# Earlier features for the next head pair, and another spacing of the background products, in a one-core diffusion layer

## The chip, the cores and the metric

One core of a Trainium2 chip. The metric is the device time of one execution in microseconds (us); less is better. TensorE does the matrix products (its clock is granted at one of two levels, 1.2 and 2.4 GHz), VectorE (DVE) and ScalarE (ACT) the elementwise work, GpSimd (POOL) some of it, and SyncE (SP) issues the transfers.

## The reference, cut to what matters

One layer for 256 latent tokens and 256 context tokens of width 2048. A wide input projection feeds two token mixers, RWKV-7 in both directions (16 heads of 64) and differential attention (8 heads); two sigmoid gates of width 2048 merge them, and a mixture of 32 experts follows.

```
px = hx @ w_in[l]                      # 3712 RWKV columns, 3072 attention columns, 4096 gate columns
S  = S * w_t - (S @ kk_t) (kk_t * a_t) + v_t k_t        # per head, forward and backward; y_t = S @ r_t
a  = softmax(q0 k0) - lam * softmax(q1 k1);  o = a @ v  # per attention head
gates = sigmoid(p_gate)
mixed = gates[0] * (y_rwkv @ w_pa) + gates[1] * (y_diff @ w_pb)
out = (silu(xb @ w1[e]) * (xb @ w3[e])) @ w2[e]         # experts, last
```

## The kernel before

The recurrence is done in chunks of 64 tokens. The 16 heads go as four pairs of pairs, q = 0 to 3; a q holds an even and an odd pair of heads (o = 0 and 1). For each q there are four stages:

- `feats`, that is `feat` for the even and then for the odd pair: loads, three small products (`pk`, `pw`, `pa`), sigmoids on ScalarE, a scan and products on VectorE and GpSimd. They give the tiles `P0`, `P1`, `R` and `kq` of the pair.
- `within`: products inside the chunks (`pc`, `px`), masked into `A` and `M`, and transposes (`pq`).
- `deltas`: first `inverse`, a substitution of 31 steps on VectorE (`prod`, then a sum into `z`), two transposes by VectorE (`ZT`, `Z`), then products of 32x32 blocks (`ph`, `pz`); beside it the side generator (transposes `pp`, `pv`, products `pb`). Then the products `pW`, `pu`, `pG`, and the chain of seven states (`pS`, then `state` on VectorE).
- `tail`: normalisation and the store of the result.

In `deltas`, `ahead(n)` emits n pieces of `feats(q + 1)`. Before, all of the next features stand behind the inverse.

All of this is the foreground. The background is one long list of weight products (L486 and L517): the attention's inputs, the keys, values and receptances (`kvr`), and at the end the gates (128 parts of 12 matmuls each, 128x128 by 128x256), then the merge with the attention's result. A weight part is loaded in 256 KB, split into `whi` (ScalarE) and `wlo` (VectorE, or GpSimd where `self.low` says so, which is during the inverse), and multiplied in 12 or 24 matmuls. Each piece of the foreground yields a weight; `interleave` multiplies it with a scale and `fill` emits background steps until their own weights (0.65 for 6 matmuls) have used it up:

```
def fill(self, us):
    self.credit += us
    while self.credit > 0 and self.at is None:
        w = self.step()
        if not isinstance(w, str):
            self.credit -= w
```

The scales are 0.936 for `diff` (the attention), 1.234 for the first `feats` and 0.444 for the four q. So a larger weight puts more background ahead of the foreground's next piece. What is emitted earlier has priority, but the framework that builds the kernel places an instruction on its engine when it takes it to be ready; the order on each engine is then fixed. Tiles with the same tag share a buffer: `b0` to `b3` hold `kq` of the even (0, 1) and of the odd pair (2, 3) and are reused in the inverse.

Of the kernel before, what the change touches and what calls it, by code (L numbers as in the profile page):

```python
# [9 lines left out]
F32 = mybir.dt.float32  # L10
# [8 lines left out]
P = 128  # L19
# [181 lines left out]
class Body:  # L201
# [793 lines left out]
    def feats(self, q):  # L995
        self.ce = self.rwt("ce", [P, 2, 2, NC], 2)

        self.vv = self.rwt("vv", [P, NC, 2, C])
        self.pts = [self.rwt(f"P{d}", [P, NC, 2, C]) for d in range(2)]
        a = yield from self.feat(2 * q)  # L1000
        b = yield from self.feat(2 * q + 1)
        return a, b
# [190 lines left out]
    def deltas(self, st, q):  # L1193

        nc, K, pt = self.nc, self.K, self.pts
        pst, tl, ident = self.pst, self.rwt, self.ident
        FW, FG, FC, FO = (0.1, 0.1, 0.1, 0.1) if q < 3 else (0.7, 0.7, 0.7, 0.7)
        W = self.rb.tile([P, 2 * NC, P], F32, tag="W", name="W")
# [9 lines left out]

        side = side()
        self.low = nc.gpsimd  # L1210
        for n, w in enumerate(self.inverse([s["A"] for s in st])):
            if n % 2:
                next(side, None)
            yield w * (1.0 if q < 3 else 0.731)
        for _ in side:
            pass
        self.low = None

        fe, nxt = (self.feats(q + 1) if q < 3 else iter(())), [None]

        def ahead(n):
            for _ in range(n):
                try:
                    w = next(fe)
                except StopIteration as e:
                    if e.value is not None:
                        nxt[0] = e.value
                    return
                if isinstance(w, str):
                    yield w  # L1230

        for dc in range(0, 2 * NC, 4):
# [23 lines left out]
        for i0, ni in ((0, 4), (4, 2)):  # L1256
            pg = [pst("pG") for _ in range(2)]
            for i in range(ni):
                for d, c in enumerate(order[i0 + i + 1]):
                    for h in range(2):  # L1260
                        for s in st:
                            o, us = s["o"], H2[1 - s["o"]]
                            n = (2 * i + d) * C
# [53 lines left out]
        for i in range(NC - 1):  # L1317
            pn = added(i + 1) if i < NC - 2 else None
            sn = state[:, (i + 1) % 4]
            if i:  # L1320
                so = state[:, i % 4]
                for h in range(2):
                    prev = None
                    for s in st:
                        o = s["o"]
                        for d in range(2):
                            n = (2 * o + d) * C
# [78 lines left out]
    def inverse(self, As):  # L1406

        nc, tl, pst = self.nc, self.rwt, self.pst
        NB = 2 * NC * 2
        Av = [A.rearrange("p d c h t -> p (d c h) t") for A in As]  # L1410

        na = tl("na", [P, 32, 32], tag="b0")
        z = tl("z", [P, 32, 32], tag="b1")
        prod = tl("prod", [P, 32, 32], tag="b2")
        rows = self.rows
        nc.vector.transpose(na.rearrange("b s t -> b t s"), self.dg16.rearrange("p d n t -> p t (d n)"))
        yield 1.5
        nc.gpsimd.memset(z, 0.0)
# [8 lines left out]
        nc.vector.transpose(ZT.rearrange("p n s -> p s n"), z.rearrange("b t s -> b s t"))  # L1427
        Z = self.rb.tile([P, NB, 32], F32, tag="s", name="Z")
        nc.vector.transpose(Z.rearrange("p n t -> p t n"), z)
        yield 3.077  # L1430

        for g in range(2):
            ph = [pst("ph") for _ in range(2)]
            for o in range(2):
                r0, r1 = rows(o, 0), rows(o, 1)
                for n in range(16):
                    m = g * 16 + n
                    nc.tensor.matmul(ph[o][r1, n * 32:n * 32 + 32], Av[o][r0, m, 32:64], ZT[r0, m, :],
                                     start=True, stop=True, tile_position=(r0.start, r1.start))
                nc.scalar.copy(H[r1, g * 16:g * 16 + 16], ph[o][r1, :].rearrange("p (n t) -> p n t", n=16))  # L1440
            yield 0.7
            pz = [pst("pz") for _ in range(2)]
            for o in range(2):
                r0, r1 = rows(o, 0), rows(o, 1)
                for n in range(16):
                    m = g * 16 + n
                    nc.tensor.matmul(pz[o][r0, n * 32:n * 32 + 32], H[r1, m, :], Z[r1, m, :],  # L1447
                                     start=True, stop=True, tile_position=(r1.start, r0.start))
                nc.scalar.copy(Av[o][r0, g * 16:g * 16 + 16, 32:64], pz[o][r0, :].rearrange("p (n t) -> p n t", n=16))
                nc.scalar.copy(Av[o][rows(o, g), :, 32 * g:32 * g + 32], Z[rows(o, g)])  # L1450
            yield 0.7

# [7 lines left out]
    def diff(self):  # L1460
# [5 lines left out]
        def tl(name, shape, bufs=1, tag=None):  # L1466
            return df.tile(shape, F32, tag=tag or name, name=name, bufs=bufs)
# [33 lines left out]
        def prepare(h):  # L1501
# [26 lines left out]
            nc.vector.tensor_tensor(flat(ro[:, 0:4, :]), flat(qk[:, 0:4, :]), ct.rearrange("p a m d -> p (a m d)"), ALU.mult)  # L1528
            yield 0.7
            nc.gpsimd.tensor_tensor(ro[:, 4:6, :].rearrange("p a (m d) -> p (a m) d", m=2),  # L1530
# [18 lines left out]
        def attend(h, qT, kT, vt):  # L1549
            oT = tl("o", [P, T])  # L1550
            for t in range(2):
                ts = slice(t * P, t * P + P)
                pm, r = [], []
                for m in range(2):
                    sc = pst("sc")
                    nc.tensor.matmul(sc, qT[:, m, ts], kT, start=True, stop=True)
                    yield 0.7
                    mx = tl("mx", [P, 1], 4)
# [4 lines left out]
                    nc.scalar.activation(p, sc, AF.Exp, scale=0.125, bias=mx, accum_out=sm)  # L1563
                    yield 0.7
                    nc.vector.reciprocal(sm, sm)
# [10 lines left out]
                nc.scalar.copy(aT, pa.rearrange("p (k q) -> p k q", k=4))  # L1576
                yield 0.7
                po = pst("po")
# [391 lines left out]
```

## Time and profile before

| | |
|---|---|
| median of 3 runs | 2506.11 us (2496.79 to 2522.02) |
| profiled execution | 2509.57 us, its span 2507.6 us, mean granted clock 0.973 |
| TensorE busy | 2346.5 us, 94% of the span |
| VectorE, ScalarE, GpSimd busy | 48%, 32%, 9% |
| attention (`diff`) | about 310 to 500 us |
| first features, then keys and values alone | about 500 to 720 us |
| q = 0, 1, 2, 3 | about 720 to 880, 880 to 1040, 1040 to 1190, 1190 to 1330 us |
| merge, output projection, router | 1330 to 1550 us |
| experts | from 1550 us on |

Busy is the share of time in which an engine has an instruction under way. The granted clock is 1 at 2.4 GHz and 0.5 at 1.2 GHz; a value between is a mean over a stretch that holds both.

### The profile page before, as it was taken

The page shows a single profiled execution, that of the slowest core. Times are in us where ns is not written, and L with a number is a line of the kernel's source. Part 1 is how long each engine was busy: PE and PEld are TensorE (multiplying, and loading weights), DVE is VectorE, ACT ScalarE, POOL GpSimd, SP SyncE. Part 2 cuts the span into 40 slices and gives each one's busy share as a digit, 9 for nine tenths or more (in the row PEclk, how much of TensorE's full clock was granted, in tenths as well). Part 3 has the DMA queues.
Part 4 walks back from the last instruction along what each step waited for, and adds up shares of the span by engine and source line. Part 5 has one row for each costly group of instructions (what it writes and reads, how often), then busy time and mean ns, then how long its engine had stood idle before and what let it go on. Part 6 is the DMA issues. An engine that isn't in the chain of part 4 may idle for free.

```text
span 2507.6 us, 45450 instructions
## 1 busy us (share of the span) xinstructions
PE 2346.5 (94%) x18419; PEld 1654.6 (66%) x18419; DVE 1204.9 (48%) x2239; ACT 796.6 (32%) x1479; POOL 219.7 (9%) x279
## 2 busy tenths in 40 slices
PE   6999989899999899999999898999999999999997
PEld 3799977788998687787899876444444434443442
DVE  3355677778655674766745654222222222222223
ACT  3332345455354655656534442000000000000000
POOL 0110012113113332102000000000000000000000
PEclk9999999999998998989889999999999999999999
DMA  9977764567754332353438897799999999999997
GB/s 348 340 243 242 238 204 138 168 206 242 231 156 124 106 115 77 122 163 100 132 116 253 257 322 273 319 421 421 420 421 421 420 421 421 421 421 421 421 421 323
DMA packets 233127, 691.50 MB, mean 276 GB/s; under 512 B 34840, under 2 KB 72400, under 8 KB 182864
## 3 DMA queue, kind: packets, MB, share of 16 engines
q1 hardware_dynamic: 232912, 688.54, 74.3%
q8 instruction: 146, 2.39, 0.4%
q14 instruction: 69, 0.57, 0.1%
HBM read 666.66 MB, written 21.78 MB: 275 GB/s over the span
## 4 chain that ended last, share of the span: by engine, by line
PE 50%; DMA 31%; DVE 8%; issue 5%; ACT 3%; POOL 2%; SPq 1%; DVEq 0%; ACTq 0%; POOLq 0%
DMA w<-in_exp_w_dram 17%; PE acc L486 12%; PE acc L517 6%; DMA r<-in_exp_w_dram 5%; PE pa L1821 5%; PE po L1856 4%; PE pt L1753 3%; PE acc L811 3%; DMA raw<-in_ws_dram 3%; DMA d<-in_exp_w_dram 2%; DVE wlo L965 1%; PE pc L1128 1%; PE ada L647 1%; PE pu L1247 1%; PE pz L1447 1%
## 5 line engine op out<-in xcount | busy, mean ns | idle before, releaser
L1821 PE MATMUL pa<-w,hg 128*64 128x512 f32 x1408 | 390.2, 596 | 35.0 <-DMA w<-in_exp_w_dram 31.8
L964 ACT CAST whi<-raw 128x512 fp32r<-128x512 f32 (+1 forms) x463 | 280.1, 614 | 310.7 <-PE acc L486 148.4
L965 DVE TENSOR_TENSOR wlo<-raw,whi 128x512 fp32r<-128x512 f32 (+1 forms) x420 | 289.4, 704 | 85.2 <-ACT whi L964 79.9
L1821 PEld LDWEIGHTS pa<-w,hg 128*64 128x64 f32 x1408 | 119.8, 137 | 245.5 <-issue 178.0
L486 PE MATMUL acc<-xr,whi 128*128 128x256 f32 (+1 forms) x1248 | 269.7, 294 | 0.7 <-ACT whi L964 0.7
L486 PE MATMUL acc<-xd,whi 128*128 128x256 f32 (+1 forms) x1248 | 267.2, 291 | 0.3 <-DVE g L750 0.2
L486 PEld LDWEIGHTS acc<-xr,whi 128*128 128x128 f32 (+1 forms) x1248 | 209.0, 195 | 20.0 <-issue 17.6
L486 PEld LDWEIGHTS acc<-xd,whi 128*128 128x128 f32 (+1 forms) x1248 | 206.3, 192 | 18.3 <-issue 14.1
L1768 DVE TENSOR_TENSOR hm<-hm,pa 128x512 f32<-128x512 f32 x16 | 11.0, 688 | 417.9 <-PE pa L1821 417.9
L1856 PE MATMUL po<-w,hT 128*64 128x512 f32 (+1 forms) x712 | 191.9, 587 | 1.6 <-DMA w<-in_exp_w_dram 0.9
L486 PE MATMUL acc<-xr,wlo 128*128 128x256 f32 (+1 forms) x624 | 182.7, 293 | 4.4 <-DVE wlo L965 3.9
L486 PE MATMUL acc<-xd,wlo 128*128 128x256 f32 (+1 forms) x624 | 181.5, 291 | 1.6 <-DVE wlo L965 1.6
L603 DVE SCALAR_TENSOR_TENSOR ada<-raw,cs,ada 128x512 f32<-128x512 f32 x180 | 136.8, 768 | 87.9 <-DMA raw<-in_ws_dram 87.6
L1875 DVE TENSOR_TENSOR acc<-acc,pt 128x512 f32<-128x512 f32 x112 | 75.3, 683 | 152.1 <-PE pt L1868 152.1
L1858 ACT ACTIVATE oh<-po,gc 128x512 fp32r<-128x512 f32 (+1 forms) x65 | 44.4, 683 | 314.9 <-PE po L1856 314.9
L1753 PE MATMUL pt<-pe,xa 128*128 128x128 f32 x1024 | 123.4, 279 | 5.9 <-DVE hg L1755 5.2
L486 PEld LDWEIGHTS acc<-xr,wlo 128*128 128x128 f32 (+1 forms) x624 | 121.5, 195 | 8.9 <-DVE wlo L965 5.7
L1753 PEld LDWEIGHTS pt<-pe,xa 128*128 128x128 f32 x1024 | 118.5, 194 | 12.1 <-DVE hg L1755 8.8
L486 PEld LDWEIGHTS acc<-xd,wlo 128*128 128x128 f32 (+1 forms) x624 | 119.7, 192 | 5.1 <-DVE wlo L965 2.4
L1856 PEld LDWEIGHTS po<-w,hT 128*64 128x64 f32 x712 | 57.6, 136 | 92.9 <-issue 87.5
L1821 PE MATMUL pa<-d,hg 128*64 128x512 f32 x304 | 109.2, 596 | 6.2 <-DMA d<-in_exp_w_dram 6.2
L1821 PE MATMUL pa<-r,hg 128*64 128x512 f32 x312 | 102.4, 596 | 7.9 <-DMA r<-in_exp_w_dram 7.9
(402 smaller groups left out, 4395.1 us busy)
## 6 DMA issues: line engine op xcount, KB each, us to landing
w<-in_exp_w_dram SPq DMA_DIRECT2D x263, 1024.0 KB
raw<-in_ws_dram SPq DMA_DIRECT2D x703, 256.0 KB
r<-in_exp_w_dram SPq DMA_DIRECT2D x58, 1024.0 KB
d<-in_exp_w_dram SPq DMA_DIRECT2D x58, 1024.0 KB
xt<-in_ws_dram SPq DMA_DIRECT2D x39, 512.0 KB
raw<-in_ws_dram SPq DMA_DIRECT2D x25, 512.0 KB
g<-gate SPq DMA_DIRECT2D x48, 128.0 KB
kvr<-own SPq DMA_DIRECT2D x16, 256.0 KB
```

Of the source, the lines that this page charges most:

```text
L486: m = nc.tensor.matmul(acc[j][:M, n * T:n * T + T], a[:, k2, j * M:(j + 1) * M], (rl if i == 1 else rh)[k], start=(k == 0 and i == 0 and s ...
L517: m = nc.tensor.matmul(acc[b][:, n * 256:n * 256 + 256], (ll if i == 2 else lh)[k][:, ts], (lo if i == 1 else hi)[:, k2, :], start=(k == 0 ...
L603: nc.vector.scalar_tensor_tensor(a, raw, c, a, ALU.mult, ALU.add)
L647: self.nc.tensor.matmul(bank[0][j, :], self.cs[:, k, :], raw[:, k - k0, :], start=(k < 4), stop=(k >= KT - 4), tile_position=(0, j.start))
L811: nc.tensor.matmul(acc[i], a[:, i * P:(i + 1) * P], b[:, k - k0, :], start=(k == 0 and q == 0), stop=(k == KT - 1 and q == 2))
L964: self.nc.scalar.copy(hi, src)
L965: (eng or self.nc.vector).tensor_tensor(lo, src, f32(hi), ALU.subtract)
L1753: nc.tensor.matmul(p[:, k * P:(k + 1) * P], xa[:, i, (k4 + k) * P:(k4 + k + 1) * P], pe[:, i, :], start=(i == 0), stop=(i == 1))
L1821: nc.tensor.matmul(a[es_, :], hg[:, k4 + k, es_], w[e][:, k, :], start=(k4 + k == 0), stop=(k4 + k == KT - 1), tile_position=(0, e * 64))
L1856: nc.tensor.matmul(o[es_, :], hT[:, f, es_], w[e][:, f, hs], start=(f == 0), stop=(f == 3), tile_position=(0, e * 64))
L1858: nc.scalar.activation(oh[:, n, hs], o, AF.Copy, scale=gc)
L1875: nc.vector.tensor_tensor(acc[:, i, os], acc[:, i, os], y, ALU.add)
```

## The change

Four things. In `deltas`, for q < 3, the features of the next even pair are emitted beside the inverse, from its yield 12 on, and finished right after it; to that end `feats` yields a mark between its pairs, and the side generator is taken at every one of the first 12 yields in place of every second. In `inverse`, the tiles move out of `b0` and `b1`, which those features need: `na` and `Z` to `b2`, `prod` to `b3`, `z` to the tag `s`. The yields between the inverse and the chain grow (3.077 to 8.0, four times 0.7 to 2.5), and those in the chain for q < 3 (0.1 each to 2.5, 2.0, 1.5 and 1.0). The pair of lines shown last for `inverse` stands behind `ph` and behind `pz`, in both passes. In `diff`, four kinds of yield go from 0.7 to 2.5: one in `prepare`, and in `attend` those behind the scores `sc`, behind the exponentials and behind the transposed weights `aT`.

```
 def feats(self, q):
         a = yield from self.feat(2 * q)
+        yield False
         b = yield from self.feat(2 * q + 1)
...
 def deltas(self, st, q):
-        FW, FG, FC, FO = (0.1, 0.1, 0.1, 0.1) if q < 3 else (0.7, 0.7, 0.7, 0.7)
+        FW, FG, FC, FO = (2.5, 2.0, 1.5, 1.0) if q < 3 else (0.7, 0.7, 0.7, 0.7)
...
-        side = side()
-        self.low = nc.gpsimd
-        for n, w in enumerate(self.inverse([s["A"] for s in st])):
-            if n % 2:
-                next(side, None)
-            yield w * (1.0 if q < 3 else 0.731)
-        for _ in side:
-            pass
-        self.low = None
-
-        fe, nxt = (self.feats(q + 1) if q < 3 else iter(())), [None]
+
+        fe, nxt, even = (self.feats(q + 1) if q < 3 else iter(())), [None], [True]
         def ahead(n):
             for _ in range(n):
+                if even[0] is None:
+                    return
                 try:
                     w = next(fe)
                 except StopIteration as e:
...
+                if w is False and even[0]:
+                    even[0] = None
                 if isinstance(w, str):
                     yield w
+
+        side = side()
+        self.low = nc.gpsimd
+        for n, w in enumerate(self.inverse([s["A"] for s in st])):
+            if n < 12 or n % 2:
+                next(side, None)
+            if n >= 12:
+                yield from ahead(1 + n % 2)
+            yield w * (1.0 if q < 3 else 0.731)
+        for _ in side:
+            pass
+        yield from ahead(100)
+        even[0] = False
+        self.low = None
...
 def inverse(self, As):
-        na = tl("na", [P, 32, 32], tag="b0")
-        z = tl("z", [P, 32, 32], tag="b1")
-        prod = tl("prod", [P, 32, 32], tag="b2")
+        na = tl("na", [P, 32, 32], tag="b2")
+        prod = tl("prod", [P, 32, 32], tag="b3")
...
+        z = self.rb.tile([P, 32, 32], F32, tag="s", name="z")
...
-        Z = self.rb.tile([P, NB, 32], F32, tag="s", name="Z")
+        Z = tl("Z", [P, NB, 32], tag="b2")
...
-        yield 3.077
+        yield 8.0
...
-            yield 0.7
+            yield 2.5
...
-            yield 0.7
+            yield 2.5
...
 def diff(self):
-                    yield 0.7
+                    yield 2.5
```

## Rows read from the trace of the kernel before

**Rows 1.** Busy time by stretch: length, PE, PEld, DVE, ACT, POOL, clock, DMA, GB/s.
```profile
310.00:500.00 190.00, 168.25 (x1171) 144.51 (x1171) 146.06 (x306) 96.83 (x226) 33.78 (x41) 0.98 0.55 171
500.00:720.00 220.00, 212.23 (x1663) 201.25 (x1662) 151.82 (x236) 102.29 (x182) 42.93 (x80) 0.99 0.70 223
720.00:880.00 160.00, 149.31 (x1908) 124.70 (x1908) 99.95 (x154) 88.04 (x155) 55.39 (x50) 0.92 0.39 116
880.00:1040.00 160.00, 152.09 (x1914) 126.43 (x1914) 101.91 (x166) 88.19 (x155) 41.33 (x39) 0.91 0.36 111
1040.00:1190.00 150.00, 144.30 (x1826) 119.27 (x1826) 99.82 (x181) 91.24 (x164) 15.43 (x19) 0.94 0.38 117
1190.00:1330.00 140.00, 139.59 (x1878) 124.36 (x1879) 85.88 (x158) 70.06 (x129) 1.42 (x3) 0.90 0.42 132
```
**Rows 2.** TensorE's waits, 310 to 500 us: total, times, longest.
```profile
PE pa L1574 <- DVE p L1570: 17.1, 11, 3.3
```
**Rows 3.** Busy time of line 486 alone, 310 to 500 us: PE, PEld, clock, DMA.
```profile
310.00:500.00 190.00, 110.66 (x814) 99.68 (x814) 0.98 0.55 171
```
**Rows 4.** The chain of waits, in order of time: start, us, what.
```profile
643.35 66.39 PE acc L486 x551
...
1035.23 3.72 PE pc L1128 x64
...
1266.36 2.04 PE ph L1438 x64
...
1283.56 2.74 PE acc L486 x13
...
1326.81 31.80 PE acc L486 x265
```
**Rows 5.** Six stretches at low clock, the last and the sum: columns of rows 1.
```profile
1272.00:1286.00 14.00, 14.00 (x152) 13.24 (x150) 1.57 (x3) 7.43 (x12) 0.00 (x0) 0.51 0.25 80
sum 100.00, PE 100.00 PEld 93.29 DVE 18.10 ACT 44.19 POOL 3.63; mean PE 16.67 PEld 15.55 DVE 3.02 ACT 7.37 POOL 0.60
```
**Rows 6.** TensorE's instructions in order of time, at two inverse ends.
```profile
786.99 1.23 PE L1438 MATMUL ph<-ZT,A 32*32 32x32 f32 x25 [3.33 <-DVE ZT L1427]
...
948.88 3.40 PE L1438 MATMUL ph<-ZT,A 32*32 32x32 f32 x64 [2.75 <-DVE ZT L1427]
```
**Rows 7.** Busy time in the substitutions of q = 0 and 2: columns of rows 1.
```profile
745.00:787.00 42.00, 38.24 (x385) 32.49 (x384) 40.31 (x65) 24.36 (x48) 21.06 (x14) 1.00 0.59 175
...
1056.00:1104.40 48.40, 47.15 (x466) 40.15 (x465) 45.83 (x90) 30.42 (x61) 0.00 (x0) 1.00 0.67 207
```
**Rows 8.** Instructions in order of time: GpSimd and VectorE in two substitutions.
```profile
757.99 1.29 POOL L965 TENSOR_TENSOR wlo<-raw,whi 128x512 fp32r<-128x512 f32 x1 [0.64 <-ACT whi L964]
...
758.26 1.41 DVE L1422 TENSOR_TENSOR prod<-z,na 128x361 f32<-128x361 f32 x1
...
1067.97 0.54 DVE L1422 TENSOR_TENSOR prod<-z,na 128x361 f32<-128x361 f32 x1
```
**Rows 9.** Groups by line, 720 to 1190 us, DVE then POOL: busy, mean.
```profile
L1062 DVE TENSOR_TENSOR_SCAN cum<-cst,ld 128x512 f32<-128x512 f32 x12 | 14.7, 1223 | 6.9 <-ACT ld L942 6.8
...
L1104 DVE TENSOR_TENSOR bon<-pcf,vv 128x256 f32<-128x256 f32 x6 | 2.5, 417 | 0.0
...
L1081 POOL TENSOR_TENSOR f<-f,k 128x512 f32<-128x512 f32 x12 | 18.6, 1550 | 1.0
...
L1068 POOL MEMSET cx<- 128x8 f32 x11 | 1.2, 112 | 9.1 <-DVE R L1092 9.1
```
**Rows 10.** TensorE in order of time: where the features of q = 2 begin.
```profile
976.07 1.13 PE L1033 MATMUL pk<-sq,cst 128*128 128x512 f32 x2
...
1006.97 1.13 PE L1033 MATMUL pk<-sq,cst 128*128 128x512 f32 x2 [0.60 <-ACT sq L1030]
```

**Rows 11.** Instructions in order of time before the substitution of q = 1.
```profile
899.96 1.99 DVE L1416 STREAM_TRANSPOSE na<-diag 128x1024 f32<-128x1024 f32 x1
...
902.79 1.68 PE L1156 MATMUL pq<-cst,kq 128*128 128x128 f32 x12
```

More of the change, by code (lines that the diff above doesn't have):

```diff
@@ L1556, in attend @@
                     nc.tensor.matmul(sc, qT[:, m, ts], kT, start=True, stop=True)
-                    yield 0.7
+                    yield 2.5
                     mx = tl("mx", [P, 1], 4)
@@ L1563, in attend @@
                     nc.scalar.activation(p, sc, AF.Exp, scale=0.125, bias=mx, accum_out=sm)
-                    yield 0.7
+                    yield 2.5
                     nc.vector.reciprocal(sm, sm)
@@ L1576, in attend @@
                 nc.scalar.copy(aT, pa.rearrange("p (k q) -> p k q", k=4))
-                yield 0.7
+                yield 2.5
                 po = pst("po")
```

## The prediction

> **What bounds the kernel now.** I read the busy times by stretch first [rows 1], then TensorE's waits and the chain of waits, then single instructions in order of time. From 310 to 1330 us TensorE is under way for 168.25 of 190, 212.23 of 220, 149.31 of 160, 152.09 of 160, 144.30 of 150 and 139.59 of 140 us [rows 1]: it idles 21.8 + 7.8 + 10.7 + 7.9 + 5.7 + 0.4 = 54.2 us, while VectorE, the next, has 146.06 of 190 in the attention and about 100 of 160 in a q. So it is TensorE's work that sets the time, not a foreground step: where the foreground makes it wait, background products mostly fill in. The change takes no product away and adds none. It can win only what TensorE loses, and there are two losses. One is the 54.2 us. The other is the granted clock, 0.92, 0.91, 0.94 and 0.90 in the four q [rows 1]. I find it in six stretches, from 787, 880, 949, 1106, 1190 and 1272 us on, together 100 us near 0.5 [rows 5], that is at 1.2 GHz. A group of 64 `ph` takes 3.40 us there [rows 6] and 2.04 us at 2.4 GHz [rows 4], so the 100 us hold 100 x (1 - 2.04 / 3.40) = 40 us of loss; 13 background matmuls in 2.74 us against 551 in 66.39 us [rows 4] say about the same (0.211 and 0.120 us each). Everything that can be won is thus 94 us. Before 310 and after 1330 us nothing changes.
>
> One unit of weight is 6 / 0.65 = 9.2 matmuls, at 0.120 us each 1.11 us.
>
> **Attention.** Of the 21.8 us, 17.1 us are eleven waits of `pa` for the weights `p` from VectorE, 1.55 us in the mean, 3.3 us the longest [rows 2]. Each yield of 2.5 in place of 0.7 puts (2.5 - 0.7) x 0.745 x 0.936 = 1.26 units, 1.4 us of products, ahead of what follows; two stand between a pair of scores and its `pa` (behind `sc`, behind the exponentials), so 2.8 us. That covers the mean wait and nearly the longest. All heads together emit 8 x 29.5 x 0.745 x 0.936 = 165 units where they emitted 8 x 11.5 x 0.745 x 0.936 = 64. The attention itself then gets longer, but the list behind it up to the first features and the keys and values shrinks by the same, and the first features no longer wait for products that were to be forced out. Bounds: 0 (the builder pulls background forward already: line 486 ran 814 matmuls there [rows 3], while 64 units are only 592) and -21.8 us. I take -14, nearer to the waits that have a name.
>
> **Features beside the substitution.** The even features leave the end of a q: two sets begin at 976.07 and 1006.97 us [rows 10], and the next `pc` stands at 1035.23 us [rows 4], so one set is 30.9 us of foreground. They enter a stretch where VectorE is the engine that sets the pace, 40.31 of 42 us and 45.83 of 48.4 us [rows 7]. Six sets between 720 and 1190 us have eleven groups on VectorE, from the scan to the last `bon`, together 83.6 us, 13.9 us a set, and six on GpSimd, 44.0 us, 7.3 us a set (of both, the first and the last row stand in [rows 9]). The 13.9 us lengthen the substitution in full. The 7.3 us matter because a `prod` that meets GpSimd waits: the same 361 elements took 1.41 us while a 1.29 us `wlo` ran on GpSimd and 0.54 us without [rows 8]. Between 0 and 7.3 us; I take 3.6. The page "SBUF — State Buffer" of the Trainium skill (section "SBUF: two separate sides") says that GpSimd and a VectorE instruction with two inputs in that memory hold their common port by an exclusive lock, for a whole instruction; the row agrees. By that rule the term would be 7.3 us.
>
> The eleven loads of a set move forward in SP's queue, among the weight loads of the inverse; at a DMA share of 0.59 to 0.67 there [rows 7] I put them at nothing. If that cover fails, a background product waits, and no step of the chain. The load of the values and the writes to `P0`, `P1` come behind the side transposes, which is what the denser side generator is for. New tile places: `na` in `b2` and `prod` in `b3` must wait for the odd pair's `pq`. In q = 1 `na` ran at 899.96 for 1.99 us while the last `pq` ended at 902.79 + 1.68 us [rows 11]; behind it, the start slips by at most 4.5 us, at least 0, I take 2. Behind `na` on VectorE stand the odd pair's mask `M` and the whole substitution.
>
> **Background put between.** The yield behind `Z` adds 4.92 x 0.444 = 2.2 units (2.4 us), the four behind `ph` and `pz` 3.2, the chain 11.9: 17.3 units or 19.2 us for each q < 3 ahead of the foreground, from 0 (had TensorE run them in those holes anyway) to 19.2.
>
> Foreground of one q: 13.9 + 3.6 + 2 + 19.2 - 30.9 = +7.8 us, between -17.0 and, with the odd features simply taking the even ones' place at the end, +44.9. It is no time yet. After the last chain 265 background matmuls follow each other for 31.8 us [rows 4]; they are a reserve. Three times 7.8 is 23 us: TensorE has work for it, so it costs nothing. Beyond 31.8 us each microsecond counts in full.
>
> **What it gives in idle time.** `ph` waited 3.33 and 2.75 us for `ZT` in q = 0 and 1 [rows 6]; 2.4 us of products ahead of it cover -4.8 us. Against that, in q = 0, with GpSimd busy for 21.06 us, TensorE lost 42 - 38.24 = 3.8 us, and in q = 2, without it, 1.25 us [rows 7]: 0.12 us for each us of GpSimd, so 3 x 7.3 x 0.12 = +2.6. Net -2, bounds -24 (all idle time of q = 0 to 2) and +22 (all 7.3 us).
>
> **What it gives in clock.** Two of the six stretches (23 us) begin with `within`, just behind the features' end; as the even features are now long there, I take half of their 9 us, -5. The other 77 us follow the 32x32 products. In q = 3 `ph` still ran at full rate with no idle time ahead, 2.04 us [rows 4], and yet at 1272 us the clock was at 0.51 with TensorE busy throughout [rows 5]: small blocks alone bring it down. Full-size products now stand between those blocks, 3.2 units or 30 matmuls in each q < 3. Whether these are enough no row shows: 0 to -31, I take a quarter, -8. Together -13. The page "TensorE: Matmul & The Clock Gate" of the Trainium skill (section "Why this matters for your kernels") asks for no idle gaps between bursts of matmuls. By that alone, closing the `ZT` waits would keep the clock in q = 0 and 1; the row of q = 3 speaks against it.
>
> **Sum.** -14 - 2 - 13 = -29 us. The profiled execution took 2509.57 us, so 2481; the median of the runs is 2506.11, 3.5 us lower, so 2477.
>
> **Rivals.**
> - *Nothing moves.* The order on each engine was made from readiness, so the background already stood where there was room; the holes that remain are where VectorE is later than planned, and they go elsewhere. For it: 814 matmuls against 592 emitted. Against it: the `pa` waits sit at one place. About 2505.
> - *Slower.* The odd features take the even ones' place behind the chain, so that the 30.9 us are not won, while the substitution grows by 13.9 + 7.3 + 4.5 = 25.7 us. Three q make 77 us; 31.8 are covered by the reserve, 45 are not; with -14 from the attention that is +31, 2537. It decides from 10.6 us of growth in each q. For it: VectorE is at 95% in the substitution. Against: the odd set starts at `pW`, with `pW`, `pu`, `pG` and seven states still to come.
> - *The clock stays up.* The products between the blocks keep it at 2.4 GHz in q = 0 to 2 and `within` starts warm: of the 40 us, all but the 14 us stretch of q = 3 (5.6) are won, -34, with 10 us of idle time in the q and the whole 21.8 of the attention: 2506 - 66 = 2440.
>
> **How the numbers follow.** Forecast 0.47 (its own range 2458 to 2495, from the terms' bounds taken half way), nothing moves 0.27, slower 0.14, clock up 0.12. To leave out no more than 2 in 10 the range goes from 2440 to 2535. One per cent (25 us) is about what a measurement of this kernel can tell, as its three runs spread over 25 us. Faster by over 1% means below 2481: a little over half of the forecast's share, all of the clock's and a trace of the second, 0.42; within it 0.42; slower 0.16, the slower case and the tail of the second.
>
> **What would show it.** In the profile after: `pa`'s waits for `p` below 5 us in all, and an attention that ends near 550 to 600 us instead of 500; `pk`, `pw`, `pa` of the features and their scan between the `prod`s; a substitution of 58 to 65 us; no wait of `ph` for `ZT` over 1 us; `within` at clock 1; a mean clock above 0.973; more than 31.8 us of unbroken background behind the last chain if the foreground got shorter, less if longer. I am wrong if `pa` still waits, if the four stretches behind the inverse stay as long at 0.5, or if the reserve is used up and TensorE waits for `state` or the tail at the end of q = 3.

## The result, and the profile after

The changed kernel takes 2527.35 us (median; 2521.14 to 2534.66) against 2506.11: a ratio of 1.0074 [1.0056, 1.0091], 18.5 us slower (the medians lie 21.2 us apart) where 29 us faster were forecast. Its profiled span is 2524.7 us at a mean granted clock of 0.968; that of before was 2507.6 us at 0.973.

Busy time by stretch, the columns of [rows 1]:

```profile
310.00:500.00 190.00, 173.30 (x1299) 159.72 (x1299) 145.13 (x281) 92.72 (x204) 31.17 (x46) 0.97 0.62 198
500.00:720.00 220.00, 201.25 (x1502) 185.78 (x1501) 158.15 (x261) 104.82 (x199) 43.55 (x73) 0.97 0.62 196
720.00:880.00 160.00, 149.16 (x1939) 126.55 (x1939) 106.90 (x168) 87.17 (x155) 40.26 (x42) 0.93 0.38 119
880.00:1040.00 160.00, 147.06 (x1933) 124.20 (x1931) 108.03 (x167) 90.08 (x158) 40.49 (x36) 0.89 0.31 96
1040.00:1190.00 150.00, 137.70 (x1814) 114.38 (x1812) 103.85 (x163) 86.54 (x154) 38.99 (x35) 0.92 0.34 105
1190.00:1330.00 140.00, 137.94 (x1796) 120.48 (x1795) 77.07 (x135) 63.98 (x121) 15.81 (x13) 0.91 0.44 144
```

TensorE idles 73.6 us in these six, after 54.2 [rows 1]. The first stretch gained 5 us of busy time, and every later one lost. GpSimd is now at work in all of the first three q (about 40 us each), where it had been nearly free in q = 2 (15.43 of 150 us).

What TensorE waits for, 310 to 1350 us: total, times, longest.

```profile
PE pa L1584 <- DVE p L1580: 27.0, 13, 4.8
PE acc L486 <- POOL wlo L965: 11.7, 5, 3.7
PE acc L486 <- ACT whi L964: 10.6, 4, 4.4
PE pcf L1104 <- DVE bon L1101: 9.0, 5, 4.1
PE pa L1057 <- DMA la<-lora: 4.0, 6, 1.8
PE pS L1293 <- DVE G L1277: 2.8, 4, 0.8
PE ph L1448 <- DVE ZT L1437: 1.9, 2, 1.1
```

The wait that was to vanish, `pa` for `p`, is longer: 27.0 us, after 17.5 us from 310 to 1350 us before (17.1 of them up to 500 us [rows 2]). Two rows in the second and third place are waits of the background itself, for the two parts of its split weights; before they were 1.1 us together. The `ZT` wait fell from 6.1 to 1.9 us.

And yet the foreground got shorter. From its first `pc` to the next q's, a q takes 147.4, 148.9 and 147.7 us (157.4, 156.9 and 154.7 before), and the last state's output stands at 1296.1 us, 17.6 us earlier. The products of line 811, behind the gates, begin 16.6 us later (1447.7 against 1431.1). So the time went to TensorE's losses, not to a late foreground step. Two columns hold them, both from 310 us to line 811 in the profiled execution: TensorE's idle time, and the time at the low clock (1.2 GHz). The median is that of all runs; the profiled execution can lie off it (e14's took 2546.80 us and e17's 2501.08, the slowest of theirs, e6's 2521.75, the fastest).

| kernel | idle us | low clock us | median us | ratio to before |
|---|---|---|---|---|
| before | 63.0 | 116.1 | 2506.11 | 1 |
| the change | 80.7 | 139.9 | 2527.35 | 1.0074 [1.0056, 1.0091] |
| e1, attention's weights alone | 67.7 | 153.6 | 2529.99 | 1.0073 [1.0044, 1.0102] |
| e4, all but those | 80.5 | 119.5 | 2520.56 | 1.0039 [1.0017, 1.0062] |

A least-squares line through the spans of the twenty profiles of this study gives span = 2409 + 0.70 x idle + 0.46 x low, no profile further than 8 us from it, over a range of 66 us. By it the change's +17.7 and +23.8 us are 12.4 + 10.9 = 23 us, of which the spans show 17. It is a line through related kernels: it says where the time stands, not why.

### The profile page after: what moved, and what is told of

Read it like the earlier page. It is cut to its first block, busy times and chain, and to the rows that moved or that the text cites. A ratio compares the mean times of both kernels' runs of the same rounds, so it can differ in the third digit from the quotient of the medians.

```text
span 2524.7 us, 45414 instructions
## 1 busy us (share of the span) xinstructions
PE 2341.4 (93%) x18419; PEld 1658.6 (66%) x18419; DVE 1225.7 (49%) x2226; ACT 795.1 (31%) x1479; POOL 238.7 (9%) x292
## 4 chain that ended last, share of the span: by engine, by line
PE 28%; DMA 25%; DVE 3%; issue 1%; ACT 0%; SPq 0%; POOL 0%; DVEq 0%; ACTq 0%
DMA w<-in_exp_w_dram 16%; PE pa L1831 6%; PE po L1866 5%; PE acc L486 4%; DMA r<-in_exp_w_dram 4%; PE pt L1763 4%; PE acc L811 3%; DMA d<-in_exp_w_dram 2%; DMA g<-gate 1%; PE pt L1878 1%; DMA gt<-mod 1%; DMA gate<-g 1%; DVE prod L1432 1%; PE pu L1257 1%; PE pz L1457 1%
## 5 line engine op out<-in xcount | busy, mean ns | idle before, releaser
L965 DVE TENSOR_TENSOR wlo<-raw,whi 128x512 fp32r<-128x512 f32 (+1 forms) x407 | 278.2, 697 | 118.5 <-ACT whi L964 110.4
L486 PE MATMUL acc<-xr,whi 128*128 128x256 f32 (+1 forms) x1248 | 280.1, 301 | 6.9 <-ACT whi L964 6.9
L486 PE MATMUL acc<-xd,whi 128*128 128x256 f32 (+1 forms) x1248 | 274.8, 297 | 4.6 <-ACT whi L964 3.7
L486 PEld LDWEIGHTS acc<-xr,whi 128*128 128x128 f32 (+1 forms) x1248 | 215.6, 200 | 27.1 <-issue 15.9
L486 PEld LDWEIGHTS acc<-xd,whi 128*128 128x128 f32 (+1 forms) x1248 | 211.4, 196 | 24.8 <-issue 17.6
L486 PEld LDWEIGHTS acc<-xr,wlo 128*128 128x128 f32 (+1 forms) x624 | 124.6, 200 | 13.9 <-POOL wlo L965 8.9
```

The source lines that it names most:

```text
L486: m = nc.tensor.matmul(acc[j][:M, n * T:n * T + T], a[:, k2, j * M:(j + 1) * M], (rl if i == 1 else rh)[k], start=(k == 0 and i == 0 and s ...
L965: (eng or self.nc.vector).tensor_tensor(lo, src, f32(hi), ALU.subtract)
```

## The experiments

Ratios are to the kernel before, run beside it on the same chip.

**The parts (e1 to e4).** Only the four 2.5s of the attention (e1); only the features beside the substitution with their tile places (e2); only the weights in inverse and chain (e3); the change without its attention weights, that is e2 and e3 together (e4).

```
e1  diff():     yield 0.7 -> yield 2.5 (4x)
e2  deltas(), feats(), inverse()'s tiles as in the change, all weights as before
e3  inverse():  yield 3.077 -> 8.0, 0.7 -> 2.5 (2x);  deltas(): FW.. = 2.5, 2.0, 1.5, 1.0
e4  the change, diff() as before
```

> The kernel before with the attention's larger yields alone. Theory A (from the traces of before and after: the first `pc` came 9.5 us later): the attention part costs 9 us, ratio about 1.004, and the waits of `pa` for `p` rise from 17 to about 25 us. Rival B (my prediction's term): it gains 14 us, ratio 0.994, and the later first `pc` is only background moved ahead.

> The kernel before with the features of the next even pair beside the substitution (with the tile places and the denser side generator), all yields as before. Theory A: this is what makes TensorE wait for `whi` and `wlo` at the end of the substitutions (22 us in the changed kernel), so it costs 10 to 15 us, ratio about 1.005. Rival B: the features are free and the larger yields are at fault; ratio 1.000 or below, since each q gets shorter.

> The kernel before with the larger yields between inverse and chain and in the chain alone. Theory A: the waits of `ph` for `ZT` go from 6.1 to below 2 us and the time falls by about 4 us, ratio 0.998. Rival B: background put ahead of the chain delays the features at the end of a q, ratio 1.003 or above.

> The changed kernel with the attention's yields put back. Theory A: the parts add up, so this is the changed kernel less 9 us, ratio to before about 1.003 to 1.004. Rival B: the attention part is a gain, so without it the kernel is slower than the changed one, ratio 1.010 or above.

Measured: e1 1.0073, e2 1.0115 [1.0087, 1.0143], e3 1.0057 [1.0036, 1.0078], e4 1.0039. Every part alone loses. Theory A held in e1 and e2, with a larger price than it gave, and in e4; in e3 its rival held. The parts don't add up: e1, e2 and e3 sum to 2.45%, the change costs 0.74%, and the attention's weights, 0.73% on the kernel before, cost 0.35% on top of e4. The weights in inverse and chain take back two thirds of what the features lose (e2 against e4). By the table, e4 lost by idle time at a nearly unchanged clock, e1 mostly by clock.

**What the attention's weights cost (e7 to e11, e15, e16).** e9, e10 and e15 set the four weights on the kernel before, one place at a time (e10 two of them). e7 puts background where none of them stands, between `p`'s last step and `pa`; e8 adds the change's weight behind `ZT`; e16 goes further; e11 gives the whole change the weight of e7.

```
                     nc.vector.scalar_tensor_tensor(pm[0], pm[0], r[0], pm[1], ALU.mult, ALU.add)
-                yield 1.0
+                yield 4.0        # e7, e8, e11;  7.0 in e16
                 pa = pst("pa")
  inverse():  yield 3.077 -> 8.0 behind ZT (e8, e16)
  diff():     yield 0.7 -> 2.5 behind ro's first half (e9), behind sc and exp (e10), behind aT (e15)
```

> The kernel before, with one number changed: the weight of background work taken between the last scaling of p and pa in the attention goes from 1.0 to 4.0. Theory: only the background that stands between that step and pa can cover TensorE's wait for p; the larger weights of the change stand elsewhere, ahead of it. Then the waits of pa for p fall from 17.5 us to below 6, and the time falls from 2506 to 2494 to 2501. Rival: the more background the attention takes, the more VectorE and GpSimd work (whi, wlo) comes into its chain, or the less is left for later stages, or the clock falls; then the time is 2506 to 2525 although the waits fall.

> As the run with 4.0 ahead of pa, and the weight after ZT raised from 3.077 to 8.0 as in the change, nothing else. Theory: both waits of TensorE (p 17.5 us, ZT 6.1 us) shrink below 6 and 2 us, and the time is 2490 to 2498, another 3 to 5 us below the run with pa alone. Rival: waits removed ahead come back as waits for the experts' or the gates' weights later, or as time at the low clock; then the time is 2503 to 2520, and the two waits have shrunk all the same.

> The kernel before, with one of the change's larger weights of the attention: 2.5 for 0.7 between the two halves of the next head's rotation (the step that leaves ro). One theory of what the attention's weights cost: the shifted rotation puts GpSimd's and VectorE's long steps beside the scaling of p (at 366.85 us of the changed kernel p stood behind ro, and ro behind a 2.98 us step of GpSimd). Then the waits of pa for p, 17.5 us from 310 to 1350 in the kernel before, rise to 22 or more and the time to 2514 or more. The rival (the weights between scores and p do it) gives 14 to 20 us of waits and 2502 to 2511.

> The kernel before, with two of the change's larger weights of the attention: 2.5 for 0.7 behind the scores and behind the exponential, the places that the prediction counted on to cover p. Theory: they stand ahead of p's last step, so they don't lengthen what TensorE has between that step and pa, and they let more whi and wlo of the background onto VectorE and ScalarE ahead of it: waits of pa for p 20 to 27 us, longer single ones (over 3.5 us), a mean clock of 0.970 or less and 2514 to 2530 us. The prediction's view, by which they are cover: waits below 10 us, and a time of 2490 to 2505.

> The changed kernel, with the weight between p's last step and pa raised from 1.0 to 4.0. Theory: it takes away the attention's part of the loss: waits of pa for p from 27 to below 12 us, the mean clock from 0.968 back to 0.971 or more, and 2510 to 2521 us, what the features cost being left. Rival: the attention's cost isn't those waits; then the waits fall and the time stays within 5 us of 2527.

> The kernel before with the last of the change's attention weights alone: 2.5 for 0.7 between pa's copy and po. Together the five weights cost 17 to 24 us; the rotation's alone cost 6 and the two at the scores 10. If the three add up, this one gives 2508 to 2518; if the loss is one of their number (background spent earlier lets more of its casts into the attention and lowers the clock), it gives 2503 to 2510.

> The best kernel so far (4.0 ahead of pa, 8.0 behind ZT: 2503.9 us), with 7.0 ahead of pa. If TensorE's remaining waits for p (8.6 us, and 5 us behind the gates' shifts on VectorE) are a matter of distance, they fall below 5 us and the time to 2496 to 2502. If the background itself puts work ahead of p on VectorE, they stay above 8 us and the time is 2501 to 2515.

Measured:

| kernel | idle us | low clock us | attention ends, us | median us | ratio |
|---|---|---|---|---|---|
| e7, 4.0 ahead of `pa` | 58.9 | 109.2 | 526 | 2508.30 | 0.9989 [0.9967, 1.0012] |
| e8, and `ZT` | 56.7 | 105.8 | 527 | 2503.89 | 0.9969 [0.9947, 0.9992] |
| e16, 7.0 | 64.8 | 126.5 | 561 | 2521.37 | 1.0054 [1.0027, 1.0081] |
| e9, rotation | 64.0 | 122.9 | 525 | 2514.27 | 1.0026 [1.0007, 1.0046] |
| e10, scores and exponentials | 70.0 | 105.8 | 577 | 2518.66 | 1.0037 [1.0020, 1.0054] |
| e15, ahead of `po` | 58.8 | 119.5 | 516 | 2509.36 | 1.0009 [0.9980, 1.0037] |
| e11, the change and 4.0 | 85.7 | 152.3 | 637 | 2533.15 | 1.0093 [1.0063, 1.0123] |

The attention ends with its last `po`, at 517 us in the kernel before. The three places add up, 0.26 + 0.37 + 0.09 = 0.72% against 0.73% in e1, each with some 0.2 to 0.3 either way. e9 needs care: `diff` takes the pieces of `prepare` for heads 1 to 7 by `next(pre)` and drops their weights, so e9 changes one weight, the first head's, and moves 1.8 x 0.936 = 1.7 units, some 16 matmuls, once. It could not shift the later rotations as its theory had it. That so small a shift goes with 0.26% means that differences of this size between these kernels can come from placement alone, and are no price of a place.

e10 holds the two weights on which the forecast built its cover. Its waits of `pa` are 16.1 us, no better than before; neither my bound for it (20 to 27) nor the prediction's (below 10) was met, and the loss shows as idle time spread over many small waits. The place between `p` and `pa` does cover. e7's waits, from 310 to 1350 us:

```profile
PE pa L1574 <- DVE p L1570: 9.3, 8, 2.2
PE ph L1438 <- DVE ZT L1427: 6.1, 2, 3.3
```

The same two in e8:

```profile
PE pa L1574 <- DVE p L1570: 8.6, 7, 2.1
...
PE ph L1438 <- DVE ZT L1427: 3.0, 3, 1.3
```

But nearly half of the wait gone gave a time that can't be told from before (e7), and in e11 the wait fell from 27.0 to 14.6 us while the time did not fall: my theory that these waits are the attention's cost fell with it. The rivals held in e7 and e8, and in e11 but for 1 us (2533.15; it allowed 2532). e16 lies above both of its ranges, and e15 lies in both of its own and decides nothing. Of the kernels that differ from before in the attention and `ZT` alone, those whose attention ends between 516 and 527 us take 2504 to 2514 us, and the three in which it ends at 561, 577 and 607 us (e16, e10, e1) take 2521, 2519 and 2530: with 7.0, e16 lost what 4.0 had won. That the later end is the cause is not shown. e9 falls between its theories, with the time of the one (over 2514) and the waits of the other (17.5 us).

**What the features cost (e5, e6, e12 to e14, e17, e18).** e5 takes the clamp out of the features' sigmoids; e6 keeps the gates' `wlo` on VectorE; e12 is e4 with e7's weight; e14 is e4 with fewer features' steps in the substitution. e18 is e4 without the `wlo` subtractions in the inverse, e13 that and no clamp, e17 the kernel before without them.

```
e5, e13   sigmoid(): no nc.vector.tensor_scalar_min(dst, dst, 1e30) for the features
e6        self.low = nc.gpsimd  ->  self.low = None
e14       yield from ahead(1 + n % 2)  ->  ahead(n % 2);  no ahead(100) behind the inverse
e13, e17, e18:
-                    self.split(t, *parts[-1], eng=self.low)
+                    if self.low is not None:
+                        parts[-1][1] = parts[-1][0]
+                        self.nc.scalar.copy(parts[-1][0], t)
+                    else:
+                        self.split(t, *parts[-1])
```

> The changed kernel, with the upper clamp on VectorE left out of the two sigmoids of the features (the limit of 1e30 on the exponential, which is not reached on these inputs). Theory: the features beside the substitution cost TensorE time because ScalarE stands in its fixed order behind that clamp (5.67 us in the one row seen) and the gates' whi casts queue behind it. Then TensorE's waits for whi (10.6 us from 310 to 1350 us in the changed kernel) fall below 4 us, and the time falls from 2527 to 2513 to 2520. Rival: VectorE and GpSimd are simply full in the substitution and the wait moves to wlo or to the features' own steps; then the sum of the waits for whi and wlo stays above 17 us (22.3 now) and the time stays within 4 us of 2527.

> The changed kernel, with the gates' wlo subtractions left on VectorE during the inverse (in the changed kernel they go to GpSimd there). Theory: wlo stands on GpSimd behind the features' steps and under the lock with VectorE's substitution steps, and that is TensorE's 11.7 us wait. Then the wait for wlo falls below 4 us and the time falls by 5 to 10 us to 2517 to 2522. Rival: VectorE is the fuller engine in the substitution, and wlo waits there as long (8.9 us of waits for a wlo on VectorE were seen with the features alone); then the waits for wlo on either engine stay above 9 us and the time stays within 4 us of 2527, or the substitution gets longer and the time rises to 2530 to 2537.

> The changed kernel with the attention's weights as before the change, and 4.0 between p's last step and pa: the change's features and weights on the best attention seen so far. Theory: the features beside the substitution cost about 10 us whatever the attention does (2520.6 without the attention's part against 2506), so the time is 2512 to 2522, above the 2504 of the same attention without them. Rival: the features' part was a loss only because the background stood in the wrong place; then it is 2495 to 2505.

> The change without its attention part (2520.6 us), with two things left out that the features and the gates' casts fight over in the substitution: the upper clamp in the features' sigmoids, and the wlo subtractions while the inverse runs (the products there read whi twice, so they are as many, and wait for whi alone). Theory: what the features cost is TensorE's wait for casts that stand behind the features' steps; with both gone the waits for whi and wlo from 720 to 1180 us fall from 18.3 us to below 4, TensorE's idle time from 310 us to the gates' end from 80.5 to below 68, and the time to 2503 to 2511. Rival: the features' own steps and the chain's wait elsewhere instead; then the idle time stays above 74 us and the time above 2514.

> The change without its attention part (2520.6 us), with a third of the features' steps beside the substitution (one at each second step of the inverse in place of one and two by turns, and the rest of the even pair beside the chain as the odd pair). Theory: the cost goes with the number of features' steps that stand among the casts, so TensorE's idle time from 720 to 1180 us falls by 4 to 9 us and the time to 2508 to 2516. Rival: where the steps stand is the same, what counts is that the foreground got shorter and its cover is spent later; then the time is within 4 us of 2520.6.

> The kernel before, with the wlo subtractions left out while the inverse runs (the products there read whi twice). A control: with the features beside the substitution, and without the clamp, the same cut gave 2481 us, 39 below. If what the features cost is their quarrel with the wlo steps, the kernel before gains little by the cut, 5 to 12 us (2494 to 2501), and without the wlo steps the features beside the substitution are a gain. If the wlo steps cost the same with and without the features, it gains 30 to 40 us (2466 to 2476), and the features are then a loss of about 10 us with or without wlo.

> The change without its attention part, with the wlo subtractions left out while the inverse runs, and the clamp kept. If the wait for whi behind the clamp matters once wlo is out of the way, it is 4 to 10 us above the 2481 of the run without both (2485 to 2491); if the clamp matters to no time, as it did with wlo in place, it is 2478 to 2485.

Measured:

| kernel | idle us | low clock us | median us | ratio |
|---|---|---|---|---|
| e5, the change, no clamp | 82.8 | 129.7 | 2527.44 | 1.0062 [1.0038, 1.0085] |
| e6, the change, `wlo` on VectorE | 86.6 | 112.6 | 2535.40 | 1.0117 [1.0078, 1.0157] |
| e12, e4 and 4.0 ahead of `pa` | 70.1 | 129.7 | 2518.69 | 1.0030 [1.0010, 1.0050] |
| e14, e4, fewer steps | 71.4 | 187.7 | 2531.67 | 1.0097 [1.0064, 1.0129] |
| e13, e4, no `wlo`, no clamp | 51.0 | 85.3 | 2481.06 | 0.9906 [0.9878, 0.9934] |
| e18, e4, no `wlo` | 51.5 | 92.2 | 2481.64 | 0.9895 [0.9867, 0.9922] |
| e17, before, no `wlo` | 50.6 | 119.5 | 2489.91 | 0.9924 [0.9894, 0.9954] |

I first took the clamp for the cause: the changed kernel showed ScalarE behind it, and the casts behind ScalarE. That theory fell. In e5 the wait for `whi` did go, the one for `wlo` stayed, and no time came of it; the two sum to 13.8 us, so its rival's mark (above 17) was missed too:

```profile
PE acc L486 <- POOL wlo L966: 12.2, 7, 4.2
...
PE acc L486 <- ACT whi L965: 1.6, 3, 0.9
```

Moving `wlo` to VectorE (e6) made the same wait 17.8 us long there, and the time longer, as the rival had it. With the better attention (e12) the features and weights still lose. Without `wlo`, e13 won 39 us against e4, more than the 8 to 18 that its theory allowed, and e18 agrees with it to 0.6 us, so the clamp has no share. But the kernel before pays for `wlo` too: the control e17 won 16 us, more than my 5 to 12 for a mere quarrel, and well under the 30 to 40 of the rival. Both hold a part, and the four kernels give its size. With `wlo` the features and the larger weights together lose 0.39% (e4); without it they win: e18 ran from 2478.44 to 2483.18 us, e17 beside it from 2485.14 to 2501.08, medians 8.3 us apart. So what was moved and `wlo` work against each other by 0.39 + 0.29 = 0.68%, 17 us, by my estimate from the intervals some 7 us either way. No run leaves `wlo` out of e2 or e3, so the times do not split the 17 us between features and weights; the idle time does, further down. Busy time from 720 to 1330 us in e4, then e17, then e18 (length, PE, PEld, DVE, ACT, POOL, clock, DMA, GB/s):

```profile
720.00:1330.00 610.00, 570.03 (x7463) 483.06 (x7462) 392.05 (x633) 329.91 (x590) 138.69 (x124) 0.92 0.38 116
```
```profile
720.00:1330.00 610.00, 594.12 (x7611) 504.30 (x7611) 377.49 (x669) 343.47 (x611) 49.98 (x67) 0.92 0.39 123
```
```profile
720.00:1330.00 610.00, 594.69 (x7743) 510.24 (x7743) 375.11 (x668) 347.37 (x622) 49.60 (x67) 0.94 0.42 130
```

TensorE idles 40.0 us in e4, and 15.9 and 15.3 in the other two, whether the features stand there or not.

e14 was missed by both theories. Its idle time fell by 9 us as the theory had it, but the low clock took 187.7 us, in the slowest of its six runs. Why fewer steps in the substitution bring that is open.

## Why the prediction was wrong, point by point

**The bound: right.** TensorE's idle time and its clock give all twenty profiled spans within 8 us. **The foreground: the size was off, to the good side.** The substitution of q = 0 grew from 40.0 to 56.6 us; 13.9 + 3.6 were forecast. But the q shrank by 10.0, 8.0 and 7.0 us where +7.8 was the sum, mainly since the 19.2 us of background put between cost next to nothing: with the weights the first three q take 473.4 us in e3 against 469.0 before, and 443.0 in e4 against 446.0 in e2. That is the term's own lower bound, by which TensorE had run products in those holes anyway. Behind the last chain 45 us of background now stand (31.8 before [rows 4]), as that reading would have it.

**`ZT`: right in size.** -4.8 forecast, 6.1 to 1.9 us measured. With the weight and without the features the wait is 3.0 us (e3, e8), and e8's median lies 4.4 us below e7's; but with the features alone it is 1.1 us (e2), so the products put ahead of `ph` are not the only thing that takes it away.

**The attention's -14: the step that failed.** Measured, the attention's weights cost 0.73% (18 us) on the kernel before and 0.35% (9 us) on top of e4. The step was this: "two stand between a pair of scores and its `pa` ... so 2.8 us. That covers the mean wait". e10 has just these two weights, and its waits of `pa` are 16.1 us where 17.5 were. What lies ahead of `pa` on TensorE covers nothing if VectorE starts `p` later by as much, as its order is fixed too. The longest wait for `p` of the changed kernel, in order of time (start, us, engine, line, operation; in brackets the idle time ahead and who ended it):

```profile
361.92 2.98 POOL L1536 TENSOR_TENSOR t<-qk,st 128x512 f32<-128x512 f32 x1 [1.32 <-DVE qk L1530]
...
363.29 0.48 DVE L1579 TENSOR_SCALAR p<-p,sm 128x512 f32<-128x512 f32 x1
364.93 1.20 DVE L1543 TENSOR_TENSOR ro<-ro,t 128x512 f32<-128x512 f32 x1 [1.16 <-POOL t L1536]
366.05 0.74 DVE L1580 SCALAR_TENSOR_TENSOR p<-p,sm,p 128x512 f32<-128x512 f32 x1
...
366.85 1.12 PE L1584 MATMUL pa<-cst,p 128*128 128x128 f32 x4 [4.77 <-DVE p L1580]
```

`p`'s last step is ready at 363.77 us but stands on VectorE behind `ro` of the next head, and that waits for GpSimd. It is the one wait of the thirteen with `ro` in that place for so long; in four more, `wlo` or steps outside the attention stand between `p`'s last two steps, for 1.2 to 1.6 us. In the kernel before that gap is never above 0.8 us. In the other eight waits `p` as a whole came late, and why is not shown. The weights did bring more products into the attention, and fewer were done in the end. Line 486 alone, changed kernel:

```profile
310.00:500.00 190.00, 136.45 (x991) 123.74 (x992) 0.97 0.62 198
500.00:600.00 100.00, 77.94 (x564) 69.94 (x563) 1.00 0.59 187
600.00:720.00 120.00, 102.90 (x770) 97.76 (x770) 0.94 0.65 204
```

The kernel before, behind [rows 3]:

```profile
500.00:600.00 100.00, 87.09 (x663) 81.48 (x664) 1.00 0.70 218
600.00:720.00 120.00, 113.53 (x918) 111.93 (x917) 0.99 0.71 227
```

177 more by 500 us, but 2325 against 2395 by 720 us, in 317.3 us against 311.3. A product brought forward into the attention took 0.138 us (136.45 / 991); behind it, it takes 0.124 (113.53 / 918), and 0.120 in the unbroken block [rows 4]. This goes with the pattern above, by which a later end of the attention is a longer time. What makes a product dearer there, beyond the clock, no run isolates.

**The features beside the substitution, +2.6: mis-sized, and the largest term.** I priced GpSimd beside the substitution by what 21 us of it had cost there in idle time [rows 7], as a slower `prod`. That reading was wrong: the 3.8 us run up to 787 us and hold the 3.33 us wait for `ZT` [rows 6], which I had booked already. From the first `prod` to the end of the last, TensorE idled 0.4 us. The same stretch in the runs:

| TensorE idle in the substitution, us | q = 0 | 1 | 2 | sum |
|---|---|---|---|---|
| before | 0.4 | 1.8 | 0.2 | 2.5 |
| e3, weights alone | 0.9 | 0.2 | 0.8 | 1.8 |
| e2, features alone | 15.4 | 9.6 | 12.7 | 37.7 |
| e4, both | 11.1 | 8.4 | 8.7 | 28.2 |
| the change | 8.7 | 9.6 | 9.6 | 27.8 |
| e6, the change, `wlo` on VectorE | 10.4 | 10.1 | 12.6 | 33.1 |
| e17, before, no `wlo` | 0.0 | 0.2 | 0.7 | 1.0 |
| e18, e4, no `wlo` | 2.7 | 2.3 | 1.8 | 6.8 |

So +25 us stand where +2.6 was forecast, above even the bound of +22. The features bring them, not the weights, and without `wlo` most are gone. q = 0 and q = 2 of the change, columns as in the first fence:

```profile
754.60:811.20 56.60, 47.94 (x404) 38.19 (x403) 53.79 (x87) 36.76 (x70) 26.69 (x22) 0.91 0.48 146
...
1051.60:1107.60 56.00, 46.44 (x399) 36.47 (x400) 53.12 (x87) 38.74 (x74) 28.06 (x23) 0.94 0.50 155
```

The features' steps meet the casts of the background there, and TensorE waits for those. The changed kernel at the end of q = 0's substitution:

```profile
785.12 0.73 ACT L941 ACTIVATE ld<-ld,c_one 128x512 f32<-128x512 f32 x1 [5.67 <-DVE ld L940]
...
791.29 2.16 ACT L964 CAST whi<-raw 128x512 fp32r<-128x512 f32 x4
791.94 0.80 PE L486 MATMUL acc<-xr,whi 128*128 128x256 f32 x2 [4.37 <-ACT whi L964]
...
794.70 7.29 POOL L965 TENSOR_TENSOR wlo<-raw,whi 128x512 fp32r<-128x512 f32 x4
796.68 0.58 PE L486 MATMUL acc<-xr,wlo 128*128 128x256 f32 x1 [2.95 <-POOL wlo L965]
798.79 2.06 DVE L1432 TENSOR_TENSOR prod<-z,na 128x784 f32<-128x784 f32 x1
799.06 0.62 ACT L964 CAST whi<-raw 128x512 fp32r<-128x512 f32 x1 [5.60 <-POOL wlo L965]
```

Four `wlo` take 1.82 us each here (one took 1.29 in [rows 8]); the next `whi` waits 5.60 us for them, and TensorE for both. All `wlo` on GpSimd from 720 to 1330 us and who waited for them; before:

```profile
L965 POOL TENSOR_TENSOR wlo<-raw,whi x43: 1270/1335/1963, 729.5 to 969.3; 128x512 fp32r<-128x512 f32 x43
...
  ACT whi L964: 1.8, 1
```

after:

```profile
L965 POOL TENSOR_TENSOR wlo<-raw,whi x56: 1261/1472/2091, 738.9 to 1224.5; 128x512 fp32r<-128x512 f32 x56
...
  ACT whi L964: 19.0, 5
```

There are 13 more, since the larger weights draw more parts into the inverse (57 in e3, 43 in e2), and the casts behind wait ten times as long. The page "SBUF — State Buffer" of the Trainium skill (section "SBUF: two separate sides") says that the shared port is locked for a whole instruction. The rows agree: the 784-element `prod` takes 2.06 us beside these `wlo`, and 1.00 us in q = 0 before. But that lock is not what TensorE waits for. In e6, with no `wlo` on GpSimd, the same `prod` takes 0.96 us in the first three q and the substitutions are some 8 us shorter each than in the change, yet TensorE idles 33.1 us in them. What e2, e3, e6 and e18 leave as the reading is that the casts stand in the fixed order of an engine behind the features' steps, on GpSimd as on VectorE.

**The clock's -13: one mechanism right, one open, the sign wrong.** `within` starts at clock 1, so the 10.2 and 13.7 us at 0.5 there in the kernel before are won. The low stretches behind the inverses of q = 0 to 2 shrank from 61.5 to 47.7 us. At 0.4 us for each that is 15 us won, where 13 were forecast. Whether the products between the blocks did the second part is open: with the weights alone those stretches are 47.7 us (e3), with the features alone 58.1 (e2), but with both and no `wlo` 58.1 again (e18). And new low stretches came with the new waits. Changed kernel, columns as in the first fence:

```profile
365.00:371.90 6.90, 5.05 (x24) 5.06 (x25) 4.62 (x7) 2.16 (x6) 0.58 (x1) 0.51 0.45 138
787.60:791.90 4.30, 0.00 (x0) 0.00 (x0) 4.26 (x7) 4.30 (x11) 1.18 (x2) 0.98 0.40 124
791.90:801.90 10.00, 7.01 (x28) 5.90 (x29) 10.00 (x9) 2.45 (x5) 9.92 (x7) 0.50 0.49 146
938.50:948.70 10.20, 6.51 (x32) 5.40 (x33) 10.20 (x9) 3.46 (x8) 10.12 (x7) 0.50 0.44 139
1245.70:1269.60 23.90, 23.90 (x277) 20.56 (x276) 2.69 (x6) 10.06 (x16) 0.00 (x0) 0.50 0.19 56
...
877.80:890.00 12.20, 12.19 (x175) 10.89 (x176) 5.75 (x9) 6.33 (x11) 0.00 (x0) 1.00 0.01 3
1174.40:1188.00 13.60, 13.59 (x185) 11.78 (x185) 6.66 (x11) 6.96 (x12) 0.00 (x0) 1.00 0.01 2
```

The kernel before, at the two starts of `within`:

```profile
879.50:889.70 10.20, 10.20 (x90) 10.08 (x89) 4.89 (x8) 4.21 (x9) 0.54 (x1) 0.50 0.32 102
1190.10:1203.80 13.70, 13.70 (x114) 13.25 (x112) 5.97 (x10) 4.91 (x10) 0.01 (x1) 0.50 0.34 115
```

In the changed kernel the first low stretch begins inside the 4.77 us wait for `p`, the third at the end of 4.3 us without a product; such stretches in the three substitutions sum to 34.0 us; before, and in e18 with its few waits there, there are none. q = 3 lost another 10.2 us (13.7 to 23.9), although its inverse has the larger weights too, at 0.731 of them, and full-size products stood between its blocks. Why e1's four q have 20 us more at the low clock than before, with no more idle time in them, is not settled.

**The rivals.** "Slower" had the sign and 2537 us, but by a longer foreground; it got shorter. The range held the time, by its slow end. Of the signs, the attention ended at 605 us, the substitutions took 56 to 58 us and `within` starts at clock 1, as said; `pa` still waited, which was named as a sign of being wrong.

## What to carry to other kernels

Filler work is not free cover: it has casts of its own, on engines that run in a fixed order, and foreground put on those engines can make the filler late; count the filler's feeders among what a moved step stands in front of. To cover a wait, put the filler between the last step of the producer and the consumer, and no more than the wait (e7, e8: 4.0 gained or held, 7.0 lost). A version with that and the `ZT` weight (e8) is the fastest that leaves nothing out, 0.9969 [0.9947, 0.9992], no larger a step than e9's, and it undoes the rest of the change. And before a stretch's idle time is taken for the price of something in it, see where the stretch ends: here it held a wait that had been counted already.

## What the runs showed of the hardware

A wait of TensorE can cost more than its length: 4.3 us without a product at 787.6 us were followed by 10.0 us at 1.2 GHz. The clock also falls with hardly a wait: in q = 3 of the changed kernel TensorE waited 1.12 us ahead of `ph` and was then busy for 23.9 of 23.9 us at 0.50, with 32x32 blocks, 64x64 products and full-size ones by turns; in the kernel before it was 14.00 of 14.00 us at 0.51 [rows 5]. And a 128x512 subtraction on GpSimd, 1.34 us in the median of the kernel before, took 1.82 us beside VectorE's two-input steps, whose 784-element `prod` took 2.06 us beside it (1.00 in the kernel before).
